# Single steps of two hand-written orders moved, one layer's buffer tables relabelled, a fourth set of weight buffers and one bank copied in the MLP

## The chip, the core and the metric

The kernel runs on one core of a Trainium2 chip. Its five engines work at the same time, each through its own queue in order: TensorE (PE in the profile, with PEld for its weight loads) multiplies matrices, VectorE (DVE), ScalarE (ACT) and GpSimd (POOL) work element by element, and SyncE (SP) starts transfers between the core's memory SBUF and the chip's main memory. TensorE writes its results into PSUM, which is used here as banks of 128 partitions by 512 numbers of four bytes. The metric is the time of one execution on the device in microseconds (us); the median of several runs counts.

## The reference

Two layers work on a sequence of 512 positions with 1024 features each, all in float32. Cut to what matters:

```python
for l in range(DEPTH):                                   # DEPTH = 2
    h = rms_norm(x, norm_mix_g[l])
    proj = h @ w_in[l]                                   # 1024 -> 3328 columns
    p_att, p_conv, p_rwkv = jnp.split(proj, [...], axis=-1)
    o_att  = diff_attention(q, k, v, lam, subln_g[l], lambda_init)   # 6 heads, causal, two softmaxes
    o_conv = short_conv(b_gate, c_gate, u, conv_w[l])                # 3 taps
    o_rwkv = rwkv7_time_mix(p_rwkv, ...)                             # 6 heads, a recurrence over positions
    x = x + jnp.concatenate([o_att, o_conv, o_rwkv], -1) @ w_out[l]
    h = rms_norm(x, norm_mlp_g[l])
    x = x + jnp.square(jax.nn.relu(h @ w_mlp_up[l])) @ w_mlp_down[l] # 1024 -> 4096 -> 1024
return rms_norm(x, final_norm_g)
```

## The kernel before

Features lie along the 128 partitions and the 512 positions along the free side, so x is eight tiles of 128 x 512, named x0 to x7. Every large product is computed to nearly float32 precision by three products of rounded numbers: a weight is split into a rounded part and its rest (whi, by a cast on ACT; wlo, by a subtraction on DVE or POOL), an activation likewise (ahi and alo), and TensorE adds whi by ahi, whi by alo and wlo by ahi in one bank. A chunk of weights is 4 blocks of 128 x 128: a tile raw arrives by a transfer from SP's queue, ACT writes whi, DVE or POOL writes wlo. The tiles rotate over a few buffers, so a transfer or a cast waits until TensorE has done with the chunk that had the buffer before.

Each layer has two stages. By the trace, layer 0's mixing runs from 0 to about 285 us, its MLP to about 623, layer 1's mixing to about 900, its MLP to about 1238; the last norm ends the program.

**Mixing.** The input projection (26 groups of columns; the bank of group g in layer l is `pjl_g`, as in pj1_24), the three mixers and the output projection are written as step sequences, one per kind of work. A string per layer, `ORDER[l]`, names by a letter whose step comes next, and `drive` plays it. This sets the order on all engines; no scheduler touches it. Letters that matter here: w casts a chunk, x and y write rests on DVE and POOL, m is one product of TensorE, e and q prepare the normalised input (ahim on ACT and alom on DVE; the squares sqm on ACT and their sum accm), R, S, r, s belong to the recurrence (pk: a projected tile taken out of its bank; zk: its shift by one position; the scans lw; phy and px: its transposes and products; vt: copies of the value tile), A, B, T and C to the recurrence's and the attention's pairs of heads (in attention, sc holds scores, ACT takes exponentials, then DVE forms a reciprocal, a scale sm and the weighted difference pp; TensorE transposes pp into ptt). One letter may issue on several engines in turn.

Where a tile has several buffers, `SLOTS[l]` says by a digit which one each tile of the stage takes, counted from where the stage before left off: `ps/mm` are two banks that the projections share with the MLP's last products; `wp/whi` and `wp/wlo` the three buffers of each part of a chunk.

**The start of layer 1's mixing** runs into the end of layer 0's MLP. The last eight products of the MLP's second projection (dn0_7_0 to dn0_7_7, one bank each in turn) are added to x0 to x7 on DVE (L1505); each new x tile is squared, scaled and split for the next norm. The norm needs the sum accm of all eight squares: TensorE adds it over the partitions by one-column products against ones (pssm), and the result scales all projections afterwards. So pj1_24 can begin before the norm is known, and pssm stands in the middle of it.

**MLP.** Here the framework's scheduler sets the order. Eight groups of columns are computed directly (`up`), the other 24, in twelve pairs, by `two`, a scheme with seven partial products (each of 12 products of TensorE with 256 columns) in place of eight, in the three banks pa, pb and pc; with two layers `two` runs 24 times. Its sums of weights (s1 to s4) are formed on DVE and split (shi_p by ACT, slo_p by DVE). The results are squared after a ReLU and feed `down`, which multiplies chunks from `weights` and adds into x. Around the place of the change:

```python
product(pa, both(s3, "p7"), smm(2), False)   # seventh of the seven, into bank pa
c1 = small("c1")
dve.tensor_tensor(c1, pa, p5, ALU.add)       # the last reader of pa
s4 = sum_("s4", w12, s2, ALU.subtract)
product(pb, both(s4, "p3"), blk(1, 1), False)
...
product(pa, both(w22, "p4"), smm(3), False)  # needs bank pa again
```

Of the kernel before, what the change touches and what calls it, by code (L numbers as in the profile page):

```python
# [22 lines left out]
S = 512  # L23
P = 128
# [38 lines left out]
         "m A2 m R3 m2 A2 m2 R3 m w x m A m2 A m5 d m4 R3 w m4 x R2 m4 d m4 g2 R2 w A2 y A m A6 m2 d m A R4 A5 m11 w y R2 m A2 m d A2 m A m r A2 R r "  # L63
         "A m4 A3 m w y R2 r h A3 R9 r d r2 m3 A2 h2 R3 m A m A3 R m2 r A2 m2 r R3 m4 w m A3 m2 R r2 y R m5 A2 r2 R2 d A m A2 r m A m2 A r m3 r3 A B "
         "w y R A B m4 R r d A2 r R3 m3 r A R r B3 r A R2 A h w r2 m2 r2 A2 m4 x d A m r2 A r m2 A3 r m2 A3 r2 m r m S A w m4 S2 y m r m r A2 d r m4 "
         "A3 m r S m w A3 m A2 m2 x m A2 m4 r m d A2 m4 S2 h w m2 A2 S m2 A x h m A2 d r2 m3 r m4 w r2 m4 y A2 m4 A r3 d m4 h S2 r S A w y A2 B2 d m3 "
         "r5 B m A2 r A S B m B A2 S B r4 m2 B m2 A2 r2 S B2 S2 m r B r2 w m2 B R2 S4 R m3 y A d m S m3 A R S2 A2 R A2 R5 m5 R3 w A3 R2 m3 A y R2 A2 "
         "m3 A R2 A2 R m3 R2 m3 d w y R3 m R2 d S R m4 S m2 S R2 m4 S2 B w y d S5 B m3 B s3 m4 A S R m5 S2 w R A S2 B y A m4 s3 R m S d A m2 B2 A m5 "
         "B3 s2 B2 w S4 s T2 s x S s S s m3 B T d B m s B2 T m4 s B m3 s2 S m3 B2 w S m2 s x m B2 m2 S2 B4 m d s B m5 B w T B m3 s S2 m B2 s2 T2 m4 "
         "B2 s m x d B T m2 B3 s2 w m2 T s m2 x m B s B m2 S T B T s T d S m3 B m2 B s B s2 T w C s2 m4 s B C3 T2 B3 m s3 m5 s B2 m C B y m3 R w y s "  # L70
         "m3 B2 m R3 d2 B T2 m S3 s m3 B S T2 m s3 w s m3 B2 S y S R2 C2 B2 C2 s2 m2 d s C T2 m2 C m2 R B C2 S2 B3 s T m C m2 s5 m4 B3 w B s C B y C "
         "s4 m3 B m d B2 m4 B2 s5 B w B2 m2 S m B3 m2 U S2 m4 S B x d B3 m3 B S B S3 w m B m2 B3 m2 B m S4 m3 B2 m4 B S2 w S B m2 S2 B3 y2 S B3 m S "
         "d2 m3 B S U2 m3 S2 m3 U B S3 B2 w S T B S3 B S T m2 T2 m3 B3 S B T B y T B2 d T2 t T2 m5 B m2 C t w m3 t T m2 y C B T C S T2 d m4 S m t3 T4 "
         "m3 w m B m T m2 x t T3 B2 m3 C3 m2 T m2 t2 C w C S m4 V T C2 t2 C2 S d T C m C S t C m3 C2 t2 C m4 t3 m w x C S C3 d m3 C3 t2 m3 t S y C m4 "
         "t m d C3 w m2 t C U t2 m C U C m x C2 d m2 t C3 m3 U m3 t2 w m3 U C2 t2 m7 C4 t2 m x U w m2 C3 d m3 t C t3 x m4 V m V m2 t C2 V t m3 d m3 C "
         "w y C m4 t C m2 d C2 t C m w m2 C m2 t3 m2 C2 T t m2 B2 m4 T4 w m C6 y t d C t T2 C2 m t m3 y U T C d C2 U T2 t2 C3 t m3 C3 t C m3 t w m2 "
         "C2 m3 t2 y T C t3 T t2 C2 m d T V S C5 S m2 t m5 t2 C2 m2 w V y m2 o m t m d C T3 V C3 m3 C5 T V2 T m2 T C m T w m2 V o m y m3 C2 T3 d m6 C "
         "w T3 o C2 T2 C T y d m3 T2 C m3 V T2 C m2 C4 m T2 m4 T w T2 C2 y C o d T m6 T4 m6 w y m o m T C m3 C m T d T m3 C m2 w m o m4 y m3 d m4 w T "
         "m4 x o T3 m2 T d m6 T w m2 o T m8 x d m3 w o m2 x m2 i m2 p m3 i d m2 w m4 o p x d i m3 p m4 w m o m3 i m3 y p2 m2 d m4 o m3 w y p m6 p d "
         "m3 w m o m3 x m2 p2 d m5 w m2 o m3 x m p2 m d m5 w m o m5 x p2 m4 i m d m4 o i m2 i w m p m3 i2 m p m2 x m2 i3 N m d w i2 m i2 m6 x N m5 w "  # L80
         "x m9 N2 m2 w y m N m34 ",
         "d3 w e x q d e w q y d w m4 x m3 d m e g m d m q m d e m w m2 q m2 y m n m d n m n m5 w m n y m n m3 d g m3 g m g m3 g w m4 x m4 d m g m2 g "
         "m3 w g m x g m4 g2 m g d g m3 g3 w m2 g2 x m3 g m6 h m d g2 m w R g4 m R2 m5 g6 m R h2 m5 g y h w m2 d m2 y d h m3 h2 m5 R m3 w x h m6 h R3 "
         "m4 d m w x m R d m3 R m2 R3 m2 R6 m3 w A m2 R2 y m4 A m4 d w R m7 R2 m5 R2 w m4 A2 x y A m4 d2 R6 r R m3 r m2 w m2 R m2 r y m8 d R5 r3 A2 "
         "R4 w m R2 m4 R A2 m3 A r x m2 R m2 A2 w m2 A2 m2 r x m3 r m2 A3 r d m2 r2 A m d r w m A2 r R m3 y r m2 R2 m2 A2 r2 A2 m R2 m d A r m w R r3 "
         "A2 R2 m2 r A2 m2 A x A R2 d r3 m2 A m2 R3 A2 r3 A r m4 A2 r2 A3 w m2 r S A m3 r2 A S2 m4 y A2 d r A r2 m4 S w A m2 A2 y m A2 m2 A2 m d m2 "
         "A2 r m4 A2 w m4 x B m A d A2 m3 A4 B m3 A m w r2 m4 A m r3 m5 A m3 A y d r3 A B2 m w y r S A2 r B S d S r3 m r A m2 S2 A2 r5 A S r m2 A S4 "
         "m2 A S2 r4 R A3 m A2 S m S m R2 A S w A m3 S m S2 R A y A2 m d m R3 m2 A2 m3 R4 m3 A w y m R3 m A2 m R m R2 m A2 d m2 R2 m2 A2 w m R2 A U y "
         "m A2 R m2 A d A3 m2 R3 S A4 S m3 R m R2 A R A S A R m3 A2 w m5 y A2 R m4 d B R A m3 R m B w A S A2 x B d m4 R m3 A2 B S4 B2 s S2 B A2 B2 A2 "
         "s R m A m2 B2 m3 S s w m3 B x A3 m4 B2 d A S R2 s2 S3 s m S R m3 R2 S5 m2 s m2 w m s2 S s m3 s m3 x w m2 A d m2 s m y m A m A B A s m2 d m3 "  # L90
         "S B2 w m2 s A S B m2 y B s m4 d S2 m B3 m2 B3 S m2 B s m3 S s2 B2 s m4 B2 w y S2 B s B2 s m2 d m C m2 s2 C w B2 m3 S2 s2 x B2 m2 s B d S2 "
         "m2 C3 m s2 B S m2 B s2 B m B2 S s w S2 s2 B2 m2 s m T s m s B2 m T3 m4 s2 m y d B m3 w B3 m4 x B3 d m4 B5 m3 s m3 w m2 s2 m T s2 m5 y B m w "
         "y m3 d2 m3 B2 T2 s T3 s5 B m2 B s3 B T10 s B m3 s4 m2 T s2 C2 m2 s3 C T B m2 B4 C w y S C2 B2 S m4 C m2 C B2 S2 d C2 B4 C B m2 w y S2 B2 S "
         "B2 m3 B2 S m d B m3 S3 B S m3 w B S3 m3 B S y S m B2 m S3 d B m B4 m2 B S m S m3 T B S2 B2 S B w B2 m2 y d S m S B T2 m B2 m3 B m3 B m3 T2 "
         "S B3 S2 B T w y B T U d T3 B t U2 B3 t T3 m5 t m2 B3 U2 B S T m5 T3 t3 w B S2 m T m2 T x d T2 m4 T t2 m3 t2 m3 w t V m2 t2 m2 x m2 t2 m2 d "
         "t m3 t w m4 B t x m d m t m3 T t2 m4 w t T2 C B2 m2 C m3 x C6 m C5 m2 C m C t d m3 t w C m2 C m t3 C x m2 C2 m2 d C t3 C2 m2 C2 m2 t m2 t C "
         "T w t2 m3 C m C2 T t T m2 t2 m C T2 y C d C m C3 m3 t m C2 U m2 w y m3 C m4 d S C2 m3 S w y U C S2 d C3 T C T C2 m t m2 C m5 t2 C T B t2 m4 "
         "T2 w C m2 t C2 m S t3 C B T3 y d C U t5 C t U m2 V2 m2 U V C2 m2 t2 m2 t C t S C3 t2 m3 C4 t m t S m2 t T w y C4 V2 T2 m3 C3 d m2 w C4 o y "
         "C3 d V m5 T5 C m3 C2 m2 C2 m T C2 T m T m C m4 T2 C w T2 m o C m3 T3 y d m2 w C V2 m y m4 T C T m C2 o m T C4 T C d V m6 C2 m2 T3 C w T3 C2 "
# [1496 lines left out]
```

## Time and profile before

| what | value |
|---|---|
| median of 3 runs | 1253.46 us (1252.2 to 1253.97) |
| the profiled execution | 1254.45 us, of which the span from the first to the last instruction is 1252.3 |
| mean granted clock of TensorE | 0.996 |
| busy, TensorE | 1234.0 us, 99% |
| busy, DVE / ACT / POOL | 915.4 (73%) / 665.7 (53%) / 374.2 us (30%) |
| memory read / written | 117.11 / 9.18 MB |

A row of the page's fifth part, of the view of waits or of a timeline names the line of the kernel, the engine, the operation and out<-in. Matmuls overlap in the records: one is still running when the next begins, so the distance of two starts, not the recorded duration, is what one costs. Line numbers in rows of before are those of the kernel before.

### The profile page before, as it was taken

What the parts mean: (1) busy time and instruction counts of PE and PEld (TensorE: products, weight loads), DVE (VectorE), ACT (ScalarE), POOL (GpSimd) and SP (SyncE); (2) the same over time, 40 slices, a digit from 0 to 9 for tenths busy, and PEclk for the clock granted to TensorE, in tenths of its full rate; (3) what the DMA queues carried; (4) which work ended last, traced back from release to release, by engine and by line L of the source; (5) the groups of instructions that cost most, each with busy time, mean ns of one, the idle gap of its engine ahead of it and who ended that gap; (6) DMA issues with size and microseconds to landing.
All of it is one profiled execution on the core that took longest, in us unless ns stands there. A gap on an engine that the chain in (4) does not pass through costs nothing. (4 is left out here: it accounts for less than half of the span.)

```text
span 1252.3 us, 24947 instructions
## 1 busy us (share of the span) xinstructions
PE 1234.0 (99%) x9493; PEld 1057.9 (84%) x9493; DVE 915.4 (73%) x1773; ACT 665.7 (53%) x1386; POOL 374.2 (30%) x461
## 2 busy tenths in 40 slices
PE   9999999999999999999999999999999999999997
PEld 6888788788899999999777887888888989898987
DVE  6787888768767676765666777887687767676754
ACT  6785655547444444444455656564583444353543
POOL 1354636333212121211225445464231111111110
PEclk9999999999999999999999999999999999999998
DMA  6523423142433333321235233332433332323122
GB/s 214 162 92 95 117 86 103 53 143 83 136 99 103 99 103 97 104 81 39 81 100 159 77 114 112 98 90 69 137 99 126 94 109 93 108 94 106 56 76 76
DMA packets 84695, 127.91 MB, mean 102 GB/s; under 512 B 21472, under 2 KB 25568, under 8 KB 84576
## 3 DMA queue, kind: packets, MB, share of 16 engines
q1 hardware_dynamic: 83856, 125.77, 32.6%
q8 instruction: 75, 1.23, 0.4%
q10 hardware_dynamic: 720, 0.55, 0.1%
q14 instruction: 44, 0.36, 0.1%
HBM read 117.11 MB, written 9.18 MB: 101 GB/s over the span
## 5 line engine op out<-in xcount | busy, mean ns | idle before, releaser
L1382 POOL TENSOR_TENSOR ml<-m,mh 128x512 fp32r<-128x512 f32 x64 | 110.3, 1739 | 481.2 <-ACT mh L1381 375.4
L338 ACT CAST whi<-raw 128x512 fp32r<-128x512 f32 x142 | 87.7, 620 | 175.2 <-PE dn L282 165.7
L282 PE MATMUL dn<-mh,whi 128*128 128x512 f32 x448 | 175.1, 391 | 0.5 <-DVE x L1505 0.5
L282 PE MATMUL dn<-ml,whi 128*128 128x512 f32 x448 | 174.8, 390 | 0.0
L282 PE MATMUL dn<-mh,wlo 128*128 128x512 f32 x448 | 174.8, 390 | 0.0
L674 POOL TENSOR_TENSOR wlo<-raw,whi 128x512 fp32r<-128x512 f32 x84 | 111.0, 1322 | 191.5 <-ACT whi L662 161.5
L282 PE MATMUL pj<-ahim,whi 128*128 128x512 f32 x392 | 157.2, 401 | 1.1 <-DVE x L1505 0.9
L282 PE MATMUL pj<-ahim,wlo 128*128 128x512 f32 x392 | 157.1, 401 | 0.0
L282 PE MATMUL pj<-alom,whi 128*128 128x512 f32 x392 | 156.4, 399 | 0.0
L1505 DVE TENSOR_TENSOR x<-dn,x 128x512 f32<-128x512 f32 x112 | 77.2, 690 | 104.7 <-PE dn L282 104.7
L662 ACT CAST whi<-raw 128x512 fp32r<-128x512 f32 x142 | 87.6, 617 | 89.7 <-PE pj L282 30.4
L339 DVE TENSOR_TENSOR wlo<-raw,whi 128x512 fp32r<-128x512 f32 x142 | 114.0, 803 | 11.4 <-ACT whi L338 9.3
L282 PEld LDWEIGHTS dn<-mh,whi 128*128 128x128 f32 x448 | 84.1, 188 | 18.1 <-issue 1.3
L282 PEld LDWEIGHTS dn<-mh,wlo 128*128 128x128 f32 x448 | 84.2, 188 | 17.8
L282 PEld LDWEIGHTS dn<-ml,whi 128*128 128x128 f32 x448 | 84.2, 188 | 16.7
L1445 ACT CAST shi_p<-s 128x512 fp32r<-128x512 f32 x96 | 59.6, 621 | 70.2 <-PE pa L282 55.3
L282 PEld LDWEIGHTS pj<-ahim,whi 128*128 128x128 f32 x392 | 74.1, 189 | 15.2 <-ACT whi L662 1.3
L282 PEld LDWEIGHTS pj<-alom,whi 128*128 128x128 f32 x392 | 74.3, 189 | 14.0 <-issue 0.5
L282 PEld LDWEIGHTS pj<-ahim,wlo 128*128 128x128 f32 x392 | 74.2, 189 | 14.0 <-DVE wlo L674 0.2
L282 PE MATMUL pa<-thi,shi_p 128*128 128x256 f32 x288 | 81.5, 283 | 0.4 <-DVE c L1491 0.4
L282 PE MATMUL pa<-tlo,shi_p 128*128 128x256 f32 x288 | 81.5, 283 | 0.0
L1446 DVE TENSOR_TENSOR slo_p<-s,shi_p 128x512 fp32r<-128x512 f32 x96 | 67.9, 708 | 18.1 <-ACT shi_p L1445 15.5
(413 smaller groups left out, 3209.7 us busy)
## 6 DMA issues: line engine op xcount, KB each, us to landing
raw<-wts SPq DMA_DIRECT2D x389, 256.0 KB, 2.7
qs<-dqhi SPq DMA_DIRECT2D x24, 128.0 KB, 3.8
ks<-dkhi SPq DMA_DIRECT2D x24, 128.0 KB, 3.8
x<-xT SPq DMA_DIRECT2D x8, 256.0 KB, 4.7
dqhi<-qhi SPq DMA_DIRECT2D x6, 256.0 KB, 3.3
dqlo<-qlo SPq DMA_DIRECT2D x6, 256.0 KB, 3.3
dkhi<-khi SPq DMA_DIRECT2D x6, 256.0 KB, 2.7
dklo<-klo SPq DMA_DIRECT2D x6, 256.0 KB, 3.6
```

The costliest lines, as they stand in the source:

```text
L282: ins = nc.tensor.matmul(*a, **k)
L338: act.copy(hi[:, :n], raw[:, :n])
L339: (pool if a and lean[0] else dve).tensor_tensor(lo[:, :n], raw[:, :n], hi[:, :n].bitcast(F32), ALU.subtract)
L662: yield act.copy(hi[:, k0:k1], raw[:, k0:k1])
L674: yield eng.tensor_tensor(lo[:, k0:k1], raw[:, k0:k1], hi[:, k0:k1].bitcast(F32), ALU.subtract)
L1382: pool.tensor_tensor(lo, m, hi.bitcast(F32), ALU.subtract)
L1445: act.copy(hi, src)
L1446: dve.tensor_tensor(lo, src, hi.bitcast(F32), ALU.subtract)
L1505: dve.tensor_tensor(x[j], pt, x[j], ALU.add)
```

## The change

Four things are changed.

1. **Steps of both orders.** In `ORDER[0]` and `ORDER[1]` some steps stand a few places earlier or later. On TensorE seven such moves come out, each of one or two projection products that now stand ahead of an instruction that waits: in layer 0 ahead of pvt, ptt, phy, px and pv, in layer 1 ahead of pssm and pvt. In layer 1 moreover the last tile's square and its sum (letter q) go ahead of its split (e), one pk goes ahead of a scan, two copies vt go ahead of two exponentials, and one zk goes behind a reciprocal, its scale and pp.
2. **Labels in `SLOTS[1]`.** The digits of `ps/mm` swap 0 and 1, those of `wp/whi` and `wp/wlo` swap 0 and 2. The pattern of sharing stays, but the first projection of layer 1 (pj1_24) takes the other of the two banks that the MLP's last products left, and its first chunk (wlo122_0 and whi122_0) another buffer.
3. **A fourth set of weight buffers in the MLP.** Every fourth chunk that `weights` loads takes raw4, whi4 and wlo4, one buffer each, from the pool that lives as long as the stage's MLP.
4. **c1.** ACT copies pa into c1, and DVE adds p5 to c1 in place, where one addition on DVE read the bank.

The arithmetic is otherwise the same; ACT has 24 copies more, no other engine's count changes.

How the rows move on the engines, at three places. First DVE at the start of layer 1's mixing: x5 to x7 are the residual adds, wlo the rests of chunks, alom the rests of the scaled tiles, accm the sum of squares, rsx the first reader of pssm. Before:

```order
L382 SCALAR_TENSOR_TENSOR alom1_5_7697<-x5_74,prm1_67,ahim1_5_7696 128x512
L1505 TENSOR_TENSOR x6_75<-dn0_7_6_7635,x6_75 128x512
L1505 TENSOR_TENSOR x7_76<-dn0_7_7_7655,x7_76 128x512
L674 TENSOR_TENSOR wlo122_0_7717<-raw122_0_7706,whi122_0_7712 128x512
L415 SCALAR_TENSOR_TENSOR alom1_6_7715<-x6_75,prm1_67,ahim1_6_7714 128x512
L430 TENSOR_TENSOR accm1_7518<-accm1_7518,sqm1_6_7719 128x512
L674 TENSOR_TENSOR wlo116_0_7738<-raw116_0_7710,whi116_0_7731 128x512
L415 SCALAR_TENSOR_TENSOR alom1_7_7747<-x7_76,prm1_67,ahim1_7_7746 128x512
L430 TENSOR_TENSOR accm1_7518<-accm1_7518,sqm1_7_7754 128x512
L359 TENSOR_SCALAR rsx_7780<-pssm1_7771 128x4
```

In the change:

```order
L680 TENSOR_TENSOR wlo122_0_7729<-raw122_0_7718,whi122_0_7724 128x512
L388 SCALAR_TENSOR_TENSOR alom1_4_7705<-x4_73,prm1_67,ahim1_4_7704 128x512
L1513 TENSOR_TENSOR x5_74<-dn0_7_5_7624,x5_74 128x512
L388 SCALAR_TENSOR_TENSOR alom1_5_7709<-x5_74,prm1_67,ahim1_5_7708 128x512
L1513 TENSOR_TENSOR x6_75<-dn0_7_6_7647,x6_75 128x512
L421 SCALAR_TENSOR_TENSOR alom1_6_7727<-x6_75,prm1_67,ahim1_6_7726 128x512
L436 TENSOR_TENSOR accm1_7530<-accm1_7530,sqm1_6_7731 128x512
L1513 TENSOR_TENSOR x7_76<-dn0_7_7_7667,x7_76 128x512
L680 TENSOR_TENSOR wlo116_0_7750<-raw116_0_7722,whi116_0_7743 128x512
L436 TENSOR_TENSOR accm1_7530<-accm1_7530,sqm1_7_7758 128x512
L421 SCALAR_TENSOR_TENSOR alom1_7_7761<-x7_76,prm1_67,ahim1_7_7760 128x512
L365 TENSOR_SCALAR rsx_7792<-pssm1_7784 128x4
```

wlo122_0 went up past alom1_4 and three residual adds; x7 went down past alom1_6 and an accm; the last accm and alom1_7 changed places. On TensorE, pssm went down by one product: of the first projection's products on x5, the third (wlo by ahim1_5), which followed pssm, now precedes it.

Second, DVE in the third attention step of a pair in layer 1. Before:

```order
L1301 ISA mx1_1_0_2_1_9595 128x1
L792 SCALAR_TENSOR_TENSOR zk2_1_9586<-pk2_1_9588,prm1_67,dk2_1_9600 128x512
L1311 RECIPROCAL sc1_1_0_2_0_9547<-sm1_1_0_2_9546 128x1
L1313 SCALAR_TENSOR_TENSOR sm1_1_0_2_9546<-s0q1_1_9368,nlam_103,sc1_1_0_2_0_9547 128x1
L1315 SCALAR_TENSOR_TENSOR pp1_1_0_2_0_9578<-sc1_1_0_2_1_9576,sm1_1_0_2_9546,pp1_1_0_2_0_9578 128x384
L674 TENSOR_TENSOR wlo103_4_9629<-raw103_4_9476,whi103_4_9620 128x512
```

In the change:

```order
L1307 ISA mx1_1_0_2_1_9607 128x1
L1317 RECIPROCAL sc1_1_0_2_0_9559<-sm1_1_0_2_9558 128x1
L1319 SCALAR_TENSOR_TENSOR sm1_1_0_2_9558<-s0q1_1_9380,nlam_103,sc1_1_0_2_0_9559 128x1
L1321 SCALAR_TENSOR_TENSOR pp1_1_0_2_0_9590<-sc1_1_0_2_1_9588,sm1_1_0_2_9558,pp1_1_0_2_0_9590 128x384
L798 SCALAR_TENSOR_TENSOR zk2_1_9598<-pk2_1_9600,prm1_67,dk2_1_9612 128x512
L680 TENSOR_TENSOR wlo103_4_9641<-raw103_4_9488,whi103_4_9631 128x512
```

zk2 went down past the three instructions that ptt waits for.

Third, DVE in layer 1's MLP, where `up` ends and the first `two` begins (slo1_8_p5 and its like are the rests of that `two`; group 139 is the last of `up`). Before:

```order
L339 TENSOR_TENSOR wlo139_0_11931<-raw139_0_11928,whi139_0_11930 128x512
L1446 TENSOR_TENSOR slo1_8_p5_12179<-s11_8_12176,shi1_8_p5_12178 128x512
L1446 TENSOR_TENSOR slo1_8_p6_12199<-s21_8_12196,shi1_8_p6_12198 128x512
L1446 TENSOR_TENSOR slo1_8_p2_12219<-raw1_8_8_4_12216,shi1_8_p2_12218 128x512
L1446 TENSOR_TENSOR slo1_8_p7_12238<-s31_8_12235,shi1_8_p7_12237 128x512
L339 TENSOR_TENSOR wlo139_4_11949<-raw139_4_11946,whi139_4_11948 128x512
```

In the change:

```order
L1397 SCALAR_TENSOR_TENSOR r1_5_11854<-up1_5_11817,rsf1_11642 128x512
L345 TENSOR_TENSOR wlo139_4_11961<-raw139_4_11958,whi139_4_11960 128x512
L1453 TENSOR_TENSOR slo1_8_p5_12191<-s11_8_12188,shi1_8_p5_12190 128x512
L1453 TENSOR_TENSOR slo1_8_p6_12211<-s21_8_12208,shi1_8_p6_12210 128x512
L1453 TENSOR_TENSOR slo1_8_p2_12231<-raw1_8_8_4_12228,shi1_8_p2_12230 128x512
L1453 TENSOR_TENSOR slo1_8_p7_12250<-s31_8_12247,shi1_8_p7_12249 128x512
```

wlo139_4, the last rest of `up`, went up past four rests of the first `two`, and wlo139_0 with it, past the sums ahead of them.

The diff; of the orders' tables a line or two is shown:

```diff
@@ ORDER[0], one line of many
-         "m A2 m R3 m2 A2 m2 R3 m w x m A m2 A m5 d m4 R3 w m4 x R2 m4 d m4 g2 R2 w A2 y A m A6 m2 d m A R4 A5 m11 w y R2 m A2 m d A2 m A m r A2 R r "
+         "m A2 m R3 m2 A2 m2 R3 m w x m A m2 A m5 d m4 R3 w m4 x R2 m4 d m4 g2 R2 w A m A y A7 m2 d m A R4 A5 m11 w y R2 m A2 m d A2 m A m r A2 R r A "
...
@@ ORDER[1], its first line
-         "d3 w e x q d e w q y d w m4 x m3 d m e g m d m q m d e m w m2 q m2 y m n m d n m n m5 w m n y m n m3 d g m3 g m g m3 g w m4 x m4 d m g m2 g "
+         "d3 w e x q d e w q y d w m4 x m3 d m q e g m d m2 d q e m w m4 y m2 n d n m n m5 w m n y m n m3 d g m3 g m g m3 g w m4 x m4 d m g m2 g m3 w "
...
@@ SLOTS[1]
-         "ps/mm 10101011010101010101001010101010101010101010 "
+         "ps/mm 01010100101010101010110101010101010101010101 "
-         "wp/whi 21021021021021021021021021021021021021021021021021021021021021021021021021 "
-         "wp/wlo 21021021021021020120120120120120120120120120120120120120120120120120120120 ")
+         "wp/whi 01201201201201201201201201201201201201201201201201201201201201201201201201 "
+         "wp/wlo 01201201201201202102102102102102102102102102102102102102102102102102102102 ")
@@ weights
     lean = [False]
+    spare, turn = [None], [0]
 
     def weights(g, k0=0, k1=NK, home=None):
 
         for a in range(k0, k1, 4):
             n = min(4, k1 - a)
-            raw = wp.tile([P, 4, P], F32, tag="raw", bufs=WB, name=f"raw{g}_{a}")
+            turn[0] += 1
+            if home is None and spare[0] and turn[0] % (WB + 1) == 0:
+                pool_, tags, bufs = spare[0], ("raw4", "whi4", "wlo4"), 1
+            else:
+                pool_, tags, bufs = wp, ("raw", "whi", "wlo"), WB
+            raw = pool_.tile([P, 4, P], F32, tag=tags[0], bufs=bufs, name=f"raw{g}_{a}")
             nc.sync.dma_start(raw[:, :n].rearrange("p k c -> p (k c)"), wts[g, :, a * P:(a + n) * P])
             if home is None:
-                hi, lo = [wp.tile([P, 4, P], F32R, tag="w" + p, bufs=WB, name=f"w{p}{g}_{a}") for p in ("hi", "lo")]
+                hi, lo = [pool_.tile([P, 4, P], F32R, tag=t, bufs=bufs, name=f"w{p}{g}_{a}") for p, t in zip(("hi", "lo"), tags[1:])]
@@ the MLP
             fp = mx.enter_context(tc.tile_pool(name=f"fp{l}", bufs=1))
+            spare[0] = fp
...
                 c1 = small("c1")
-                dve.tensor_tensor(c1, pa, p5, ALU.add)
+                act.copy(c1, pa)
+                dve.tensor_tensor(c1, c1, p5, ALU.add)
...
                 last_group(fp, wbase, mids)
+            spare[0] = None
```

66 rows, old and new, of the table ORDER are left out of this document.

## The prediction

> **What bounds the kernel now.** I read the page first, for the engine that is full; then the waits of TensorE, since only its gaps can be won back; then windows by stage; then the timelines of the engines around the longest gaps.
>
> ```profile
> span 1252.3 us, 24947 instructions
> PE 1234.0 (99%) x9493; PEld 1057.9 (84%) x9493; DVE 915.4 (73%) x1773; ACT 665.7 (53%) x1386; POOL 374.2 (30%) x461
> ```
>
> TensorE is busy for all but 18 us, so an edit that leaves its instructions as they are can win little. Its own waits, from the view of waits filtered to PE (total us, times, longest us):
>
> ```profile
> PE pssm L282 <- DVE accm L430: 1.6, 1, 1.6
> PE ptt L287 <- DVE pp L1315: 1.4, 2, 1.2
> PE pj L282 <- DVE x L1505: 0.9, 1, 0.9
> PE pbv L282 <- ACT vt L881: 0.6, 1, 0.6
> PE up L282 <- DVE wlo L339: 0.6, 1, 0.6
> PE px L282 <- DVE yi L1161: 0.5, 1, 0.5
> PE pa L282 <- DVE c L1491: 0.4, 1, 0.4
> PE pvt L287 <- DVE vf L1269: 0.3, 1, 0.3
> PE pv L282 <- DVE zv L792: 0.3, 1, 0.3
> PE phy L287 <- DVE ysum L1101: 0.2, 1, 0.2
> PE pj L282 <- DVE pk L787: 0.2, 1, 0.2
> ```
>
> These rows are what the change can touch. The rest of the 18 us is the start, the end (after 1238 us) and waits that it leaves alone. By stage (start:end and length, then busy time of PE, PEld, DVE, ACT, POOL, then TensorE's granted clock, DMA share and GB/s):
>
> ```profile
> 450.00:612.00 162.00, 162.00 (x994) 145.98 (x993) 111.17 (x183) 70.80 (x126) 25.36 (x17) 1.00 0.27 84
> 612.00:640.00 28.00, 25.02 (x108) 19.64 (x107) 17.26 (x22) 12.70 (x22) 11.00 (x12) 0.94 0.32 100
> 640.00:900.00 260.00, 257.85 (x2654) 212.60 (x2652) 195.60 (x448) 153.72 (x377) 118.37 (x181) 1.00 0.35 106
> ```
>
> The MLP shows no gap in its last 162 us. The turn from layer 0's MLP into layer 1's mixing has 3 us of gaps in 28 us, and a granted clock of 0.94. That is the first place.
>
> **The turn, 612 to 640 us.** TensorE (start, us, instruction, idle before it):
>
> ```profile
> 622.20 0.39 PE L282 MATMUL dn<-mh,wlo 128*128 128x512 f32 x1
> 623.49 0.47 PE L282 MATMUL pj<-ahim,whi 128*128 128x512 f32 x1 [0.91 <-DVE x L1505]
> ...
> 627.10 0.39 PE L282 MATMUL pj<-ahim,whi 128*128 128x512 f32 x1
> 627.32 0.39 PE L282 MATMUL pj<-alom,whi 128*128 128x512 f32 x1
> 629.31 1.05 PE L282 MATMUL pssm<-ones,accm 128*128 128x1 f32 x8 [1.60 <-DVE accm L430]
> ...
> 632.08 0.63 PE L282 MATMUL pj<-ahim,wlo 128*128 128x512 f32 x1
> 632.51 0.63 PE L282 MATMUL pj<-ahim,whi 128*128 128x512 f32 x1
> ```
>
> A 512-column product is recorded as 0.39 us, but the next starts 0.23 later (627.10 to 627.32), so a wait costs 0.16 more than its row shows: the first one 1.07, the second 1.76. Behind the second, products start 0.43 apart (632.08 to 632.51): a stretch at half clock. The window's clock of 0.94 lacks 6% of 28 us, 1.7 us: a stretch of some 3.4 us at half speed, in which half the work was left undone. DVE and POOL in the same place:
>
> ```profile
> 622.07 1.27 DVE L1505 TENSOR_TENSOR x<-dn,x 128x512 f32<-128x512 f32 x2
> 623.27 0.68 DVE L674 TENSOR_TENSOR wlo<-raw,whi 128x512 fp32r<-128x512 f32 x1
> ...
> 625.27 1.66 DVE L674 TENSOR_TENSOR wlo<-raw,whi 128x512 fp32r<-128x512 f32 x1
> 626.85 0.74 DVE L415 SCALAR_TENSOR_TENSOR alom<-x,prm,ahim 128x512 fp32r<-128x512 f32 x1
> 627.51 1.75 DVE L430 TENSOR_TENSOR accm<-accm,sqm 128x512 f32<-128x512 f32 x1
> ```
> ```profile
> 624.79 1.59 POOL L674 TENSOR_TENSOR wlo<-raw,whi 128x512 fp32r<-128x512 f32 x1 [3.19 <-ACT whi L662]
> 627.37 1.33 POOL L674 TENSOR_TENSOR wlo<-raw,whi 128x512 fp32r<-128x512 f32 x1
> ```
>
> The same DVE operation takes 0.68 alone and 1.66 when it starts inside POOL's; it ends 0.55 us after POOL does (626.38 and 626.93), and so does accm (628.70 and 629.26). The order after the change has four gains here. The first product of pj1_24 takes the bank of dn0_7_6, not dn0_7_7, so it waits for one residual add of the pair at 622.07: 622.85, my estimate (622.07 + 0.69 + a handover of 0.1), for 623.49. Eighteen products stand before pssm where seventeen did; at the old pace TensorE is through them at 627.1. The rest wlo122_0 (0.68) leaves the stretch for a gap further up, and accm7 stands before alom7 (0.74), its square being first on ACT. Against them, the last residual add now follows alom6 and accm6, so it comes at about 624.9, not 622.7, and its square at about 626.1. Then wlo116_0 ends at 626.2 to 626.8 (alone, or behind POOL's first operation) and accm7 at 627.4, or at 628.2 if POOL's second operation, then 0.3 earlier, catches it. So pssm starts at 627.5 to 628.3 for 629.31, with one product more done: **a gain of 1.2 to 2.0; I take 1.6**, the middle, as each of the two collisions can go either way.
>
> The half clock came after 1.6 us of idling and 0.9 of one-column products. The wait of 1.2 for ptt, in the window from 640 to 900 us with its clock of 1.00, was followed by none. With 0.4 to 1.2 us left before pssm (627.5 to 628.3, less 627.1), which the view would show as 0.2 to 1.0, I take it as gone: **1.7**, with nothing as the other bound.
>
> The Trainium skill, in "TensorE: Matmul & The Clock Gate" (Part 1, the HAM clock gate), says that the gate halves the clock after about one idle window of 3.4 us and that these windows run freely. The length of the stretch agrees; that only 2.5 us of idle and near-idle time called it does not. By the idle rule alone the old wait would have cost no clock and the term would be 0; by the free windows, whether a shorter wait still calls it is a matter of phase, which is the third rival.
>
> **The attention step in layer 1 (one step T).** DVE, POOL, and TensorE's last product before ptt, which then starts at 765.89:
>
> ```profile
> 763.08 1.77 DVE L792 SCALAR_TENSOR_TENSOR zk<-pk,prm,dk 128x512 f32<-128x512 f32 x1 [1.60 <-POOL pk L788]
> 764.77 0.16 DVE L1311 RECIPROCAL sc<-sm 128x1 f32<-128x1 f32 x1
> 765.22 0.62 DVE L1315 SCALAR_TENSOR_TENSOR pp<-sc,sm,pp 128x384 f32<-128x384 f32 x1
> ```
> ```profile
> 763.01 1.29 POOL L674 TENSOR_TENSOR wlo<-raw,whi 128x512 fp32r<-128x512 f32 x1
> ```
> ```profile
> 764.29 0.39 PE L282 MATMUL pj<-alom,whi 128*128 128x512 f32 x1
> ```
>
> Reciprocal, scale and pp were queued behind zk, which itself stood behind POOL. They go first now and take 1.07 (764.77 to 765.84). If they start at 763.0 pp ends at 764.1, before TensorE wants it at 764.52; zk still ends at about 764.9, because POOL held it until then anyway. Gain 765.89 less 764.52 = 1.37; if POOL also slowed pp, by the 0.55 above, still 1.3. **1.3.**
>
> **Other steps in layer 1.** The first pk goes ahead of a scan: the row is 0.2 + 0.16 = **0.3** to 0.4. The wait for pvt in layer 1 is too short for a row, so one product ahead of it covers at most the 0.16 of the overlap: **0.1**. The two vt copies ahead of the exponentials would win the 0.6 + 0.16 of pbv, but put the exponentials as much later and with them ptt, just behind pbv: **0**, between a gain of 0.7 and a loss of 0.3.
>
> **Layer 0.** One or two products (0.23 each) go ahead of five waits. The one ahead of pvt writes the bank that vf, the wait itself, is reading: **0**. The others, capped by 0.23 a product: ptt 0.24 (the smaller of two in 1.4), phy 0.23, px 0.46, pv 0.38 of 0.47, sum 1.3. The first three lie where the next DVE result is due soon after, so part returns: **0.8**, between 0.2 and 1.3.
>
> **The MLP.** Two rows count, up and pa.
>
> ```profile
> 355.89 0.69 DVE L1451 TENSOR_TENSOR s<-raw,raw 128x512 f32<-128x512 f32 x1 [0.88 <-DMA raw<-wts]
> 356.50 0.42 DVE L1491 TENSOR_TENSOR c<-pa,p 128x256 f32<-128x256 f32 x1
> ```
> ```profile
> 940.03 1.77 DVE L1446 TENSOR_TENSOR slo_p<-s,shi_p 128x512 fp32r<-128x512 f32 x1
> ```
> ```profile
> L1474 ACT COPY p<-pa x24: 350/367/368, 349.9 to 1188.3; 128x256 f32<-128x256 f32 x24
> ```
> ```profile
> 378.09 0.62 ACT L1445 CAST shi_p<-raw 128x512 fp32r<-128x512 f32 x1 [0.80 <-PE pb L282]
> ```
>
> The add c1, the last reader of bank pa, waited behind a sum that waited for a transfer. A copy on ACT now frees the bank; its price is that of the other copy out of pa, 0.37. The wait of 0.4 + 0.16 goes: **0.5**, 0.2 if the transfer holds something else too. In a repetition without that wait ACT idles 0.80 before 378.09, where the copy falls, until the product in pb is done; after that p4 needs the bank. So the copy is free with 0.43 to spare, and 24 x 0.37 = 9 us of ACT are hidden there. The add that stays on DVE now reads two tiles of SBUF and can stand behind POOL as slo_p does at 940.03 (1.77 for 0.68); r, m and the products of down come much later, and cover the 1.1.
>
> With the fourth set of weight buffers one chunk is cast ahead, and wlo139_4 stands in front of the four slo_p that it followed. The wait of up (0.6 + 0.16) goes: **0.7**; 0.3 if DVE, full here, is late with the next rest. The extra casts fall before the MLP; one behind a late transfer would hold ACT's queue, for some 0.6 at most (one cast's 0.62): the lower bound of this edit is 0.
>
> **Sum.** 1.6 + 1.7 + 1.3 + 0.3 + 0.1 + 0 + 0.8 + 0.5 + 0.7 = 7.0. Of the 5.3 apart from the clock I let 1.6, three tenths, return as waits at the next place (a choice: about the terms of layer 0 and up, where DVE is fullest): 5.4. The profiled execution was 1254.45 (span 1252.3 and 2.15 around it), 1.0 above the median of 1253.46; so 1249.05 for such an execution, 1248.1 against the median: **1248.2**, rounded to the safe side. With every term at its top (2.0, 1.7, 1.4, 0.4, 0.2, 0.7, 1.3, 0.6, 0.7 = 9.0, and 1 returned) it is 1245.5; with every term low and no clock won (1.2, 0, 1.0, 0, 0, -0.3, 0.2, 0.2, 0.3, less 0.6 for the cast) it is a gain of 2.0: 1251.5.
>
> **Rivals.**
> 1. *Absorbed.* TensorE's gaps of a few tenths are set by DVE's chains, and DVE's work is the same; every step won is waited for at the next one. For it: DVE is 73% busy and nearly full at 622 to 629. Against: the MLP behind each mixing stage has no gaps to take the gain up, so what reaches it stays won. Only T, pa and half of the turn would remain, less 1.6: 1.3 + 0.5 + 0.8 - 1.6 = 1.0, or 1252.5.
> 2. *Slower: the copy of c1.* ACT works in order. If a cast (0.62) and an activation of about the same length stand before the copy where the 0.80 was idle, the bank comes 1.24 later, 0.43 of it covered: p4 waits 0.8. Half of the 24 steps have such activations beside them by my estimate: 9.6 us, less some 4 of the forecast's 5.4 that remain: 1259. It decides from the point where more than 0.43 of ACT's work moves into that gap. Against: the gap opens in each repetition by PE's pace, and only 0.37 enters it.
> 3. *The half clock stays*, or falls elsewhere: all other terms hold, 1249.9. For it: the one instance in the trace gives no threshold, and the one-column products stay in any case. Against: the wait of 1.2 for ptt that called none.
>
> **How the numbers follow.** Forecast 0.54, half clock stays 0.20, absorbed 0.16, slower 0.10. This kernel's measurement tells 0.2%, 2.5 us, from no change. Faster by more needs a time under 1251.0: 0.50 of the forecast, 0.18 of the third rival, 0.03 of the first, 0.71. The same: 0.20, from the first and the tails. Slower: 0.09. The forecast's own range is 1245.5 to 1251.5; to leave out 2 in 10 at most it reaches over the first rival: 1245 to 1252.8.
>
> **What would show it.** In the profile after: pssm's row at 0.2 to 1.0 or gone, and a clock of 1.00 in the window of the turn; ptt's longest wait at 0.2; the rows for up and pa<-c gone; pvt<-vf still 0.3. It is wrong if a wait of pa on the copy shows up some twenty times, if the sum of TensorE's waits falls and the span doesn't, or if the half clock appears at another place.

## The result, and the profile after

| | median | range | runs |
|---|---|---|---|
| before | 1252.72 us | 1251.87 to 1253.97 | 6 |
| after | 1245.84 us | 1245.61 to 1248.23 | 6 |

The ratio is 0.9948, 95% interval 0.9935 to 0.9961: faster, by 6.9 us between the medians. Repeated later on another chip, beside 24 runs of before, it was 1246.75 (1245.62 to 1250.39, 7 runs) for 1251.12: 0.9962, interval 0.9948 to 0.9977, 4.4 us between the medians. (A ratio with its interval is worked out from all runs; it need not be the quotient of the two medians.) So faster is certain; how much depends on which executions of before are met, and the experiments show why.

The changed kernel's page, and those of its waits of TensorE that bear on the change (total us, times, longest us):

```profile
span 1244.0 us, 24981 instructions
PE 1230.9 (99%) x9493; PEld 1055.0 (85%) x9493; DVE 912.8 (73%) x1773; ACT 675.2 (54%) x1410; POOL 373.4 (30%) x461
```
```profile
PE pot L287 <- DVE ot L1347: 0.8, 1, 0.8
PE ptt L287 <- DVE pp L1321: 0.8, 2, 0.5
PE dn L282 <- DVE x L1513: 0.5, 2, 0.3
PE pj L282 <- DVE vf L1275: 0.4, 1, 0.4
PE pssm L282 <- DVE accm L436: 0.4, 1, 0.4
PE pj L282 <- DVE x L1513: 0.3, 1, 0.3
```

The span fell by 8.3 us and TensorE's busy time by 3.1, with the same 9493 instructions: overlap and clock, not work. The rows for up, pa<-c, pbv, px<-yi, phy and pv are gone. The row pssm that is left is layer 0's, at 21 us; the one at the turn is gone. The longest wait for ptt is 0.5, where the prediction's sign was 0.2; it stands behind pbv, which no longer waits:

```profile
683.14 0.33 PE L287 MATMUL ptt<-cst,pp 128*128 128x128 f32 x1 [0.52 <-DVE pp L1321]
```

To find where the 8.3 us went I took the start of each TensorE product in one trace less the start of the same product in the other (the median over those within 1.5 us of a place). What changes from one place to the next was won there:

```
place (time in before)              won, profile to profile
the start, to 30 us                 0.27   (differs by up to 1.9 among the profiles here)
layer 0, 30 to 283 us               0.0    (with the start, 0.5 ahead at 148, 0.2 at 180)
layer 0's MLP, at 320 us            0.1
pa, at 357 us                       0.64
turn, 622 to 640 us                 3.6
pk, at 647 us                       0.47
pvt, at 680 us                      0.26
pbv and ptt, at 688 us              0.70
T, at 765 us                        1.43
end of layer 1's mixing             -0.2
up, at 942 us                       0.88, of which 0.4 is lost by 960
pa, at 1017 us                      0.29
the end                             0.3
```

The turn after the change, TensorE, then DVE, then POOL, then the window with its clock:

```profile
621.86 0.47 PE L282 MATMUL pj<-ahim,whi 128*128 128x512 f32 x1 [0.34 <-DVE x L1513]
...
625.86 0.40 PE L282 MATMUL pj<-ahim,wlo 128*128 128x512 f32 x1
626.22 1.05 PE L282 MATMUL pssm<-ones,accm 128*128 128x1 f32 x8
...
628.37 0.39 PE L282 MATMUL pj<-ahim,wlo 128*128 128x512 f32 x1
628.60 0.39 PE L282 MATMUL pj<-ahim,whi 128*128 128x512 f32 x1
```
```profile
624.38 1.18 DVE L680 TENSOR_TENSOR wlo<-raw,whi 128x512 fp32r<-128x512 f32 x1
625.48 0.68 DVE L436 TENSOR_TENSOR accm<-accm,sqm 128x512 f32<-128x512 f32 x1
```
```profile
623.58 1.43 POOL L680 TENSOR_TENSOR wlo<-raw,whi 128x512 fp32r<-128x512 f32 x1 [3.02 <-ACT whi L668]
624.95 0.95 POOL L804 MEMSET ad<- 128x1024 f32 x1
626.33 1.64 POOL L680 TENSOR_TENSOR wlo<-raw,whi 128x512 fp32r<-128x512 f32 x1 [0.42 <-ACT whi L668]
```

```profile
612.00:640.00 28.00, 27.17 (x123) 21.18 (x122) 17.87 (x25) 16.44 (x28) 11.12 (x12) 1.00 0.32 107
```

pssm follows the product ahead of it at once. The last sum took 0.68 where it had taken 1.75: it was through (626.16) before POOL's second rest began (626.33). Products behind pssm start 0.23 apart, not 0.43, and the window has a clock of 1.00: no half clock. This trace runs about 1.05 us ahead of before's when the turn begins.

### The profile page after: what moved, and what is told of

It is laid out like the page before. It is cut to its first block, busy times and chain, and to the rows that moved or that the text cites. A ratio compares the mean times of both kernels' runs of the same rounds, so it can differ in the third digit from the quotient of the medians.

```text
span 1244.0 us, 24981 instructions
## 1 busy us (share of the span) xinstructions
PE 1230.9 (99%) x9493; PEld 1055.0 (85%) x9493; DVE 912.8 (73%) x1773; ACT 675.2 (54%) x1410; POOL 373.4 (30%) x461
## 3 DMA queue, kind: packets, MB, share of 16 engines
q8 instruction: 74, 1.21, 0.4%
## 4 chain that ended last, share of the span: by engine, by line
PE 91%; DVE 3%; ACT 2%; POOL 1%; issue 1%; DMA 1%; SPq 0%; POOLq 0%; ACTq 0%; DVEq 0%
PE dn L282 23%; PE pj L282 20%; PE pa L282 11%; PE po L282 8%; PE up L282 7%; PE pb L282 6%; PE dnF L282 3%; PE pc L282 3%; PE sc L282 1%; PE ptt L287 1%; PE pg L282 1%; PE pyy L282 1%; PE pzw L282 1%; PE pst L282 1%; PE pap L282 0%
```

## The experiments

The times are medians, the ratio is against the kernel before on the same chip in the same hour. "Ahead" is the comparison of starts described above, against the profile of before.

**Layer 0's five moves alone.** The table `ORDER[0]` of the change, everything else as before:

```diff
-  ORDER[0] of before
+  ORDER[0] of the change (pvt, ptt, phy, px and pv, each with one or two products ahead of it)
```

> The kernel before with the five moves of layer 0 alone. The prediction's step: 0.8 us won, 1251.9 for a median before of 1252.7. The rival, absorbed: what the moves win up to about 150 us (0.2 to 0.5) is waited for again by 220 us, so 0, the starts of TensorE at 250 us within 0.3 of the kernel before, and the wait for pv comes back at the ptt behind it.

1252.28 us for 1251.70, ratio 1.0006 (0.9994 to 1.0019). TensorE is 0.1 behind before at 45 us and 0.1 ahead at 250 us. In the changed kernel it can be seen what became of the wait for pv; TensorE's timeline there:

```profile
218.72 0.40 PE L282 MATMUL pj<-alom,whi 128*128 128x512 f32 x1
219.36 0.33 PE L287 MATMUL ptt<-cst,pp 128*128 128x128 f32 x1 [0.25 <-DVE pp L1321]
```

No wait stands before pv any more, and 0.25 + 0.16 = 0.41 stands before ptt, about 2 us later: what pv's two products won (0.38), ptt gives back, since its pp comes from DVE at its own time. phy's 0.23 and px's 0.1 were given back by 180 us. The product moved ahead of pvt waits for vf itself (the row pj<-vf, 0.4, where pvt<-vf was 0.3). All five moves together are worth 0.2 in this kernel's profile, 0.0 in the changed kernel's, and nothing in the times: absorbed.

**The turn alone**: steps and labels.

```diff
 ORDER[1]
+ the last tile's q (square, sum) ahead of its e (split); one product ahead of pssm
 SLOTS[1]
+ ps/mm with 0 and 1 swapped, wp/whi and wp/wlo with 0 and 2 swapped
```

> The kernel before with the turn alone: square and sum ahead of the split, one product ahead of pssm, and the labels of the two banks and of the weight buffers. If the wait and the half clock both go: 1.9 to 2.1 for the waits and 1.7 for the clock, 3.6 to 3.8 us, 1249.0. If the half clock has to do with something else (its phase): 2 us, 1250.7, and a window with a clock under 1 within 10 us of pssm in some of the runs.

1249.60 for 1251.70, 0.9981 (0.9970 to 0.9992). In its profile TensorE wins 3.6 us from 622 to 640 us, no wait stands before pssm, and the window from 600 to 650 us has a clock of 1.00. The profile agrees with the first theory, the median of 2.1 us with the second. This contradiction the next experiments take up.

**The two edits of the MLP alone.**

```diff
+ every fourth chunk of weights in raw4, whi4, wlo4
-                dve.tensor_tensor(c1, pa, p5, ALU.add)
+                act.copy(c1, pa)
+                dve.tensor_tensor(c1, c1, p5, ALU.add)
```

> The kernel before with the MLP's two edits alone, the fourth buffer set and the copy of c1. Forecast by the terms: pa 0.5 and up 0.7, with the small wait of layer 1's pa 0.2 more: 1.2 to 1.5 us, 1251.3. The rival that is slower: p4 waits for the copy in many of 24 steps, 2 us or more lost, and a row of waits of pa on an ACT copy.

1248.86 for 1251.70, 0.9984 (0.9973 to 0.9995). In the MLPs TensorE wins 0.64 and 0.29 at pa and 0.88 at up, less 0.36: 1.45, as the terms said. But it also wins 2.7 us from 622 to 640 us, where no step was moved. DVE, POOL and TensorE there:

```profile
626.39 0.68 DVE L433 TENSOR_TENSOR accm<-accm,sqm 128x512 f32<-128x512 f32 x1
```
```profile
626.38 1.81 POOL L677 TENSOR_TENSOR wlo<-raw,whi 128x512 fp32r<-128x512 f32 x1 [0.23 <-ACT whi L665]
```
```profile
627.12 1.05 PE L279 MATMUL pssm<-ones,accm 128*128 128x1 f32 x8 [0.52 <-DVE accm L433]
```

The two began within 0.01 us; this time POOL waited (1.81 for some 1.28) and DVE did not. So the last 1.07 of the wait for pssm in before is a race between accm and a rest on POOL, and the half clock came with the long form of the wait: here the clock from 600 to 650 us is 1.00. POOL's start waits here for the cast ahead of it on ACT, and the cast 0.46 for its transfer; in before that cast waits 0.29 for TensorE.

**The buffer set alone**, with c1 as before:

```diff
+ every fourth chunk of weights in raw4, whi4, wlo4
```

> The kernel before with the fourth set of buffers alone, c1 as before. If that set carries what the MLP's two edits brought at the turn and the wait of up: TensorE ahead by 0.9 at up, pssm's row 0.5 with a clock of 1.00, the rows of pa<-c still there (0.64 and 0.29 lost). If c1 carried it: the turn and up as before.

1249.82 for 1251.12, 0.9994 (0.9982 to 1.0006): the times alone show no change. In the profile TensorE wins 0.88 at up, 0.65 at 357 us (there without the copy: the transfer came in time), and 2.7 at the turn, where pssm's row is again 0.5 and the clock 1.00; accm began 0.02 behind POOL's rest and took 0.68. At 1017 us it loses 0.5, and its waits still hold the row of c1:

```profile
PE pa L279 <- DVE c L1495: 0.6, 1, 0.6
PE pssm L279 <- DVE accm L433: 0.5, 1, 0.5
```

The wait at up is gone in every profile with the fourth set; of the kernels without it only one, the steps of the turn without the labels, was without that wait (it won 0.6 there). So up belongs to the buffers. The wait at pa needs the copy to be gone for certain; at 1017 us the kernels that leave c1 alone lie between 0.5 lost and 0.3 won, so the changed kernel's 0.29 there may be the execution's. (Lines of the experiments are those of their own kernels; 282 is written there as 279 or 282, with the length of the order's text.)

**The race itself.** In before, the rest that POOL forms next to the last accm is formed on DVE, behind that accm:

```diff
 LO[1]
-  "xyxyyxxx..."
+  "xyxxyxxx..."
 ORDER[1]
-  "... m w m2 q m2 y m n m d n ..."
+  "... m w m2 q m2 x m n m d n ..."
```

> The kernel before with one rest moved: wlo116_4, which POOL forms and which starts 0.14 us ahead of the last accm in the kernel before, is formed on DVE behind that accm. If the wait for pssm is 1.07 of collision with POOL (accm 1.75 for 0.68) and the half clock hangs on that wait: pssm's row falls from 1.6 to 0.5, no clock under 1 behind it, 2.8 us won, 1249.0. If the collision isn't it: the row stays at 1.6 and the time too.

The profile does what the first theory says. DVE, TensorE, and the window from 600 to 650 us:

```profile
628.53 0.68 DVE L427 TENSOR_TENSOR accm<-accm,sqm 128x512 f32<-128x512 f32 x1
```
```profile
629.27 1.05 PE L279 MATMUL pssm<-ones,accm 128*128 128x1 f32 x8 [0.57 <-DVE accm L427]
```
```profile
600.00:650.00 50.00, 47.79 (x214) 38.14 (x213) 34.34 (x45) 29.45 (x49) 14.24 (x16) 1.00 0.30 97
```

TensorE wins 2.7 us from 622 to 640, for one rest moved. But the median is 1250.53 for 1251.08, 0.9990 (0.9980 to 0.9999): 0.6 us, not 2.8. What it took away is the upper part of the times: 1249.97 to 1251.71 for 1250.00 to 1254.97.

**Before, once more**, unchanged:

> The kernel before once more, unchanged, for a second profiled execution. If the late accm and the half clock are a race of 0.14 us that falls either way: in executions near 1250 pssm's row is 0.5 to 0.9 and the clock 1.00, in those at 1252.5 to 1255 it is 1.6 with the half clock, and the profile shows one of the two, by its own time. If they belong to the program: 1.6 and a clock of 0.97 from 600 to 650 us whatever its time.

1251.38 us, from 1249.95 to 1254.94 in 12 runs. The profiled execution was one of 1254.10. DVE, POOL, TensorE, window:

```profile
627.45 1.76 DVE L427 TENSOR_TENSOR accm<-accm,sqm 128x512 f32<-128x512 f32 x1
```
```profile
627.40 1.26 POOL L671 TENSOR_TENSOR wlo<-raw,whi 128x512 fp32r<-128x512 f32 x1 [0.19 <-ACT whi L659]
```
```profile
629.27 1.05 PE L279 MATMUL pssm<-ones,accm 128*128 128x1 f32 x8 [1.59 <-DVE accm L427]
```
```profile
600.00:650.00 50.00, 46.77 (x202) 37.31 (x201) 33.55 (x43) 27.48 (x47) 15.46 (x17) 0.97 0.29 94
```

The same wait and the same half clock, with POOL 0.05 ahead (0.14 in the profile of the prediction). Layer 0's moves, and the other four moves in layer 1 below, leave the turn as it was, and both their profiles show it too: waits of 1.60 and 1.62, a clock of 0.97 from 600 to 650 us. I have no profile of the old turn without it.

But each execution's mean granted clock is known, and a stretch of 3.4 us at half speed takes 0.0014 from it. The half clock at the end of the program, from which the profiles lose between 2.1 us (the clock of 0.89 from 1230 to 1249 us of the other four moves) and 4.0 us (0.79, the turn alone), takes 0.0017 to 0.0032 more. As long as the end lies in these bounds, a mean of 0.998 leaves no room for the stretch, 0.996 or less has it, and 0.997 can be either. Of 98 executions of before on three chips, 29 had 0.996 or less, with a median of 1253.49 us; 28 had 0.997 and 41 had 0.998, with medians of 1250.78 and 1250.84. So the half clock is a matter of the execution, and the profile that the prediction was worked out from (1254.45 us, 0.996) is one that has it. That the race falls the other way in the shorter executions is argued, not seen in a trace: the two groups lie 2.7 us apart, which is the wait and the half clock together (1.07 + 1.7) and not the clock alone. Why all four profiles of the old turn show the long form, when by the clocks 29 to 57 of 98 executions do, stays open.

**The steps of the turn without the labels, and the labels without the steps.**

```diff
 first kernel: ORDER[1] as in the turn alone, SLOTS[1] of before
 second kernel: ORDER[1] of before, SLOTS[1] as in the turn alone
```

> The turn's steps without the labels: the last square and sum ahead of the split, one product ahead of pssm, banks and buffers as before. If the steps carry the gain: pssm's row at 0 to 0.5 and a clock of 1.00, 2.5 us or more; the first product of pj1_24 still waits, and now for a later add: 2 us more in its row than the 0.9 before would take it all back, so 0 to 2.5 us in all, 1249.5 to 1252. If the labels carry it: 0.

> The labels alone, no step moved. By the banks: the first product 0.6 earlier, but pssm comes when the last sum does, so the wait moves behind it: pssm's row at 1.5 to 2.2, half clock as before, 0 won. By the chance of the collision with POOL: if the two meet otherwise, pssm's row at about 1 and the half clock gone, 2.8 us won.

Steps alone: 1249.99 for 1251.08, 0.9982 (0.9973 to 0.9992), ten executions within 1.4 us. pssm starts without a wait; the first product still waits 0.94 for the later bank, as in before, and not longer as I had feared, since with the old labels x6 and x7 are still added one behind the other. TensorE wins 3.2 us from 622 to 640. The collision has moved: POOL's rest (628.43) now meets alom, which takes 1.80, and nothing on TensorE waits for that at once.

Labels alone: 1250.45 for 1251.08, 0.9987 (0.9978 to 0.9997). The first product's wait falls from 0.91 to 0.32, and what it wins comes back before pssm:

```profile
628.62 1.05 PE L279 MATMUL pssm<-ones,accm 128*128 128x1 f32 x8 [0.85 <-DVE accm L427]
```

accm begins (627.88) 0.19 before POOL's rest (628.07) in this profile and takes 0.68, but two of its ten executions have a clock of 0.996. So the steps make the turn safe in these executions, and the labels win the rest of the wait, 0.6; each alone is worth some 3 us in its profile, and both together 3.6.

**The other four moves in layer 1.**

```diff
 ORDER[1]
+ R (pk) ahead of a scan; one product ahead of pvt; R R (vt copies) ahead of the exponentials; T (zk) behind pp
```

> The kernel before with the other four moves of layer 1 alone: pk ahead of a scan, one product ahead of pvt, the vt copies ahead of the exponentials, zk behind pp. The prediction's terms: 0.3 + 0.1 + 0 + 1.3 = 1.7 us. By the whole change's profile, in which TensorE is 0.5 ahead behind the first, 0.7 behind the copies and 1.4 behind zk: 2.7 us, 1250.0, if each is worth by itself what it is worth in company.

1248.73 for 1251.70, 0.9976 (0.9965 to 0.9988). In the profile: pk 0.47, pvt 0.26, the copies 0.14, T 1.40: 2.3 us, between the 1.7 and the 2.7 of the expectation; the median, 3.0 lower, is above both. Its turn is the old one, and its ten executions fall in two groups, seven from 1247.37 to 1248.80 us and three from 1250.52 to 1251.19; the profiled one is the slowest, with the half clock:

```profile
600.00:650.00 50.00, 46.97 (x205) 37.49 (x204) 33.64 (x43) 28.07 (x48) 15.48 (x17) 0.97 0.30 94
```

The copies' 0.70 in the changed kernel isn't theirs. In kernels that leave those copies alone TensorE wins at the same place 0.5 (layer 0's moves), 0.6 (the MLP's edits), 0.9 (the buffer set), 1.1 (the turn, the one rest, the steps, the labels), and before's second profile, after losing 0.8 just ahead, 1.0. With the copies moved it wins 0.14 here, 0.70 in the changed kernel's first profile and 0.2 in its second, so what the move is worth can't be told from these. The profile of before had an unlucky wait there. The cast that stands ahead of the copies on ACT waited 3.22 us for its transfer in before; with the turn alone it waited 1.60, for a product.

T's price isn't fixed either. In three kernels that leave zk where it was (the MLP's edits, the steps of the turn, the buffer set) the wait for ptt is 0.46, 0.48 and 0.60, where before has 1.21, and TensorE wins 0.6 to 0.7 there without the move. In the MLP's edits:

```profile
760.62 0.55 PE L284 MATMUL ptt<-cst,pp 128*128 128x128 f32 x3 [0.46 <-DVE pp L1318]
```

zk in the changed kernel, DVE, then TensorE:

```profile
757.37 0.62 DVE L1321 SCALAR_TENSOR_TENSOR pp<-sc,sm,pp 128x384 f32<-128x384 f32 x1
757.90 0.74 DVE L798 SCALAR_TENSOR_TENSOR zk<-pk,prm,dk 128x512 f32<-128x512 f32 x1
```
```profile
758.24 0.39 PE L282 MATMUL pj<-alom,whi 128*128 128x512 f32 x1
758.47 0.49 PE L287 MATMUL ptt<-cst,pp 128*128 128x128 f32 x3
```

zk takes 0.74 behind pp, where it took 1.77 ahead of it, because POOL is done by then; pp isn't slowed by POOL; ptt comes 0.23 after the product ahead of it: no wait.

**The copy of c1 three times**, in the changed kernel:

```diff
                 act.copy(c1, pa)
+                act.copy(c1, pa)
+                act.copy(c1, pa)
                 dve.tensor_tensor(c1, c1, p5, ALU.add)
```

The framework's scheduler also moved a few rows of the MLP for it.

> The changed kernel with the copy of c1 made three times, one after the other (0.37 each). By the spare time of 0.43 that the prediction worked out for ACT: 0.74 more is 0.3 over, in each of 24 steps, 7 us slower than the changed kernel, 1253. By the rival that the copy is already at its limit: 0.74 x 24 = 18 us slower, 1264. If ACT has more to spare than that: no slower, 1246.

1253.34 us, 6.6 over the changed kernel's later median (on another chip). From 357 us to 610 TensorE falls back by 3.0 against before, from 1020 to 1235 by 2.5, some 0.23 for each of the 24 steps. The wait shows on the weight loads of TensorE:

```profile
PEld pa L279 <- ACT c L1497: 7.5, 22, 0.3
```

22 waits of a third of a microsecond each for 0.74 more: ACT had 0.74 - 0.34 = 0.4 to spare by these waits, 0.5 by TensorE's loss, for the prediction's 0.43. The way to lose by this edit exists, and one copy is clear of it.

**A version beyond the change.** The changed kernel without layer 0's move ahead of pvt, and with three output products ahead of the transposes pot, the largest wait that the change leaves in the middle of the program:

```diff
 ORDER[0]
- "... T w T2 C2 y C o d T m6 ..."
+ "... T w T2 m3 C2 y C o d T m3 ..."
```

> The changed kernel without layer 0's move ahead of pvt, and with three output products ahead of the transposes pot in layer 0, which wait 0.8 for ot. By the terms 0.8 + 0.1: 0.9 us under the changed kernel. By what became of layer 0's other moves (absorbed by the next result of DVE within 20 us): TensorE is 0.5 to 0.7 ahead behind pot, and level with the changed kernel again at 283 us.

The changed kernel itself ran beside it:

> The changed kernel again, beside the other three on one chip. If the half clock is gone from all its executions, they lie within 2 us of each other, and 5 to 6 us under the median before, since some of the executions before do without the half clock too. If the first comparison's 6.9 holds for any chip: 6.5 to 7.5.

1245.62 us (1245.08 to 1247.35, 6 runs) beside the changed kernel's 1246.75 and before's 1251.12: 0.9953 (0.9938 to 0.9968) against before. It is 1.1 under the changed kernel, by medians of 6 and 7 runs whose ranges overlap. In the profiles TensorE's lead over the changed kernel grows by 0.72 at pot, from 0.22 to 0.94, and stays between 0.93 and 1.16 to the end, so the gain is not absorbed. TensorE at pot:

```profile
245.06 0.40 PE L279 MATMUL po<-mhi,whi 128*128 128x512 f32 x1
245.34 0.63 PE L284 MATMUL pot<-cst,ot 128*128 128x128 f32 x4
```

No wait is left. My second expectation, absorbed like the rest of layer 0, was wrong here. In the second comparison, the changed kernel kept its times within 1.5 us in six of seven executions; the seventh was 1250.39 with a clock of 0.996, so a half clock may still fall somewhere; no profile shows where.

## Why the prediction was right, and where not

The time, 1245.84, lies in the range of 1245 to 1252.8, 2.4 under the forecast of 1248.2; the way and the order of the gain were as forecast. By its steps:

- **The turn: right in its place and mechanism.** pssm's wait was forecast at 0.2 to 1.0 or gone; it is gone. The sum comes earlier than I had worked out, 626.16 here, or 627.2 in the time of before, for 627.4 to 628.2, since neither collision cost its full price. With the clock the turn won 3.6 in the profile for 1.6 + 1.7 = 3.3.
- **The half clock: gone, as taken; its price was mis-sized for the median.** The step that failed is in the sum: I subtracted 1.7 (and the 1.07 of the late accm) from one profiled execution and carried the gain over to the median whole. In 29 of 98 executions of before, 57 at most, the clock was lost; in the median, by the times, it wasn't. The kernel with one rest moved puts a number to it: 2.7 in the profile, 0.6 in the median. The first comparison hid this, as its six runs of before had a median of 1252.72.
- **T: right in its mechanism**, 1.4 for 1.3 against the profile of before; against the three kernels with the shorter wait it is 0.7 to 0.8, so here too one profile's wait was taken for all; why it was shorter there stays open. **pk**: 0.47 for 0.3. **pvt in layer 1**: 0.26 for 0.1.
- **The vt copies: the mechanism as said.** pbv's wait of 0.58 is gone and a wait of 0.52 stands before ptt (1.08 with the other four moves alone). The sum's 0 fits the 0.14 that they bring there; the 0.7 in the changed kernel's first profile may be that of the place. The sign that ptt's longest wait would be 0.2 left out this very wait.
- **Layer 0: wrong.** The term of 0.8 is 0 to 0.2 by the profiles. The cap of 0.23 a product was applied move by move; the next result of DVE was not looked up for each of them. The product ahead of pvt waits for vf, as said.
- **The MLP: right.** pa 0.64 for 0.5, and perhaps 0.29 in layer 1, for which the sum has no term; up 0.88 for 0.7, with 0.4 returned by 960 us. The copy is free: no wait on it stands in the changed kernel's waits.
- **The allowance of 1.6 for gains that return**: layer 0's 0.8, 0.4 behind up and 0.2 at the end of layer 1's mixing are 1.4. As a size it was right; I had put it down to layer 0 and up.
- **The baseline.** The profiled execution was 1.0 above the median then known, and 3.6 above the 1250.81 of those executions of before with a mean clock of 0.997 or 0.998. Counted from these, the change wins 1250.81 - 1246.75 = 4.1 us. The profiles give 8.3; without the 1.07 and the 1.7 it is 5.5, and without the 0.5 to 1.1 that kernels with the copies in their old place win at 688 us as well, 4.4 to 5.0. The forecast without the 1.07 and the 1.7 is 5.4 - 2.8 = 2.6. So the turn was priced too high for the median and the rest, layer 0 aside, too low; that the forecast gain of 5.3 lies between the 6.9 and the 4.4 of the two comparisons is in part luck.

The rivals: slower by the copy was shown possible, from 0.4 us of ACT's time on, and did not come about. Absorbed was right for layer 0 alone. A half clock that stays, or falls elsewhere, may be what one execution of seven had (1250.39 us, mean clock 0.996).

The Trainium skill's page "TensorE: Matmul & The Clock Gate" (Part 1) lets the clock fall after about 3.4 us of idling. Here it fell behind 1.6 us of idling and 0.9 us of one-column products in all four profiles that have that wait, and in none of those with 0.9 or less at that place, so in this case the measured stretches decide.

## What to carry to other kernels

A wait that one profile shows may belong to that execution: where a race of a tenth of a microsecond, a late transfer or a dip of the clock stands behind it, look at the spread of the times, at each run's mean clock and at a second profile before the gain is put at its full size. A product moved ahead of a wait wins only if the next result isn't due at its own time anyway, so for each move look up the wait behind it, up to the next stretch without any. Before work goes to another engine in a tight loop, measure that engine's idle time where the work will stand: it told here to within a tenth what would be free (0.43 for 0.4 to 0.5).

## What the runs showed of the hardware that I had not expected

- Where accm on DVE, with two inputs from SBUF, and a rest on POOL start almost together, one holds the other up, and a few hundredths of a microsecond decide which: with POOL 0.05, 0.14 and 0.20 us ahead DVE waited (1.76, 1.75 and 1.75 for 0.68), with POOL 0.01 and 0.02 ahead POOL waited (1.81 and 1.82 for some 1.28). These cases fit an order by start, with a turning point between 0.02 and 0.05 in the recorded times.
- A MEMSET on POOL did not hold DVE up: in the changed kernel accm began at 625.48, inside a memset from 624.95 to 625.90, and took its 0.68.
- The half clock outlasts its cause: behind a wait of 1.6 us with 0.9 us of one-column products after it, it lasted some 3.4 us in all four profiles that have it and took 1.7 us more.
